# Pieces of eviction queued by step, an output product begun inside attention, and three buffers for the merge rows

## The chip, the cores and the metric

The kernel runs on one core of a Trainium2 chip. The core has five engines that work side by side and wait for each other by semaphores: TensorE (PE in the profile, its weight loads PEld), VectorE (DVE), ScalarE (ACT), GpSimd (POOL) and SyncE (SP), which here only issues DMAs, in order. The metric is device time of one execution in microseconds. Before the change the median of three runs is 2999.45 us (2996.9 to 3003.93).

## The reference

A trunk of two post-norm layers over a sequence of 1024 rows of width 1024, batch one, in float32. Each layer has a token mixer and then an MLP; each of these four sub-layers computes, for its input x,

```
h = x * (1 + scale) + shift          # shift, scale, gate from a conditioning vector c
x = LayerNorm(ALPHA * x + gate * f(h)) * ln_g + ln_b
```

The four functions f are, in order: a gated spatial mixer (`mixer_a`), an MLP `square(relu(h @ w_up)) @ w_down` with an inner width of 4096, attention (`mixer_b`), and a second MLP. Attention has 16 heads of 64 and three dilated patterns; each pattern gives an output and the logarithm of its softmax sum, and the three outputs of a head are added with the softmax of those logarithms as weights:

```
wts = softmax(stack(lses), axis=0)[..., None]
o = sum(wts * stack(outs), axis=0)
return o.reshape(B, S, H * E) @ w_out
```

## The kernel before

**Arithmetic.** Every float32 operand of a product is split into a rounded part and a rest (`split`, lines 102 and 103: a copy, mostly on ScalarE, then a subtraction, mostly on VectorE), and each product is three matmuls: hi·hi, hi·lo, lo·hi. A matmul has 128 rows of contraction, 128 columns of weights and up to 512 moving columns. A weight is loaded, multiplied by the gate row where it is an output weight (GpSimd, line 337), and split; that is a `unit`.

**Order of the work.** The program is written out in one order. The tile framework then orders the instructions of each engine by a simulated run with a cost for each, lowest position in the program first among those that are ready; an instruction can so be placed ahead of ones written before it, except those marked by `tc.keep_in_program_order`. Buffers come from pools: a tag has so many buffers, and a new tile waits until the old tile of its buffer has been released. SyncE's DMAs run in the order of its queue, and a DMA that waits for its source or its buffer holds those behind it.

**Output products** (`out_rows`, `rows_half`). The products of both mixers, `mixer_a` and attention, go through `out_rows`. The contraction of 1024 is cut in four chunks of two units, and the rows in two halves, which gives eight parts of 8 groups of 6 matmuls. The order of the parts (chunk, half) is (0,0), (0,1), (1,0), (1,1), (2,0), (3,0), (2,1), (3,1). A group of the first chunk is copied to the accumulator rows `acc` by ScalarE (line 367), a later one is added by VectorE (line 369). `add_x` adds the residual, `finish` does the LayerNorm of a row tile. The last part is interleaved with the building of the next sub-layer's input.

**MLP** (`mlp`). Both products use a scheme of seven half-size products in place of eight, numbered 1 to 7. The down products run in the order 2, 1, 5, 6, 3, 7, 4, each in eight steps of 24 matmuls. A step's operands are loaded (`load_step`, lines 861 and 872; one or two tiles of 512 KB from five buffers, two tagged `raw` and three tagged `res`) and split (`prepare`) into tiles from 13 buffers; the loads run two steps ahead and the splits one. Products 2, 5 and 3 accumulate in one set of four PSUM banks, 1, 6, 7 and 4 in another. After a product's last step its four banks are evicted at once (`evict`, lines 911 to 932): copies on ScalarE after 2, 5 and 6; on VectorE an addition (926), a multiplication by the gate (927) and an addition to the accumulator (930) after 1, 3 and 7; after 4 a multiplication (923) and an addition. After 3 and after 4 a row tile is complete and `finish` follows: statistics (240, 241), the reciprocal root (229 to 235), the normalization on ScalarE (245, 246), and for the MLPs the affine part with `ln_g` and `ln_b`: in the first MLP by GpSimd for six rows and VectorE for two (303, 304), in the second by GpSimd or VectorE (310 to 316), and a store (320). Product 4 ends row by row: its last two steps (four in the second MLP) are done for one bank after the other.

**Attention** (`attention`). `project` yields the projections q, k and v of 24 pairs (eight head pairs, three patterns) matmul group by matmul group; these are TensorE's filler. The attention itself stands in a table of 200 slots with three positions each, eight slots per head pair and pattern: scores, softmax, transposes and weighting. After each position two pieces of the projections follow. The projections end in slot 183; the last pattern occupies slots 184 to 191. `merge` combines the three patterns of a head pair: it reads the statistics back, computes the factors (1244 to 1256), writes them out, and reads them as rows broadcast over 64 partitions each (1272). The three rows of a merge share one buffer tagged `lng`, but in the last merge two have a tile of their own. Each is used to scale an output as soon as it is there (1273; on GpSimd for two of them, for one in the last merge), and two additions follow two slots later (1277, 1278). `attention_out` then opens its pools, loads the gate row (250), and calls `out_rows`; seven of the eight pairs' outputs come back from DRAM, the last is used where it is.

Of the kernel before, what the change touches and what calls it, by code (L numbers as in the profile page):

```python
# [10 lines left out]
F32 = mybir.dt.float32  # L11
F32R = mybir.dt.float32r
AF = mybir.ActivationFunctionType
ALU = mybir.AluOpType
# [22 lines left out]
def trunk(ctx: ExitStack, tc: tile.TileContext, x, c, ada_w, ada_b, ln_g, ln_b, a_w_in, a_b_in,  # L37
# [217 lines left out]
    class Residual:  # L255
# [3 lines left out]
        def __init__(self, j, stack):  # L259
            self.j = j  # L260
            halves = [pool(stack, f"acc{j}_{half}", 1, side="right") for half in (1, 0)][::-1]
            self.acc = [halves[i // 4].tile([P, D], F32, name=f"acc_{j}_{i}") for i in range(NT)]
            self.hT = []

# [22 lines left out]
        def finish(self, i):  # L287
# [7 lines left out]
            if j in (0, 2):  # L295
                nc.sync.dma_start(spill[j][i * P : (i + 1) * P, :], z)
            if j in (1, 3):
                if i == 0:
                    self.affine(j)
                xo = work.tile([P, D], F32, name=f"xo_{j}_{i}", tag="res", bufs=3)  # L300
                if j == 1:
                    e = G if i < 6 else V
                    e.tensor_tensor(xo[:], z, self.g[:], op=ALU.mult)
                    e.tensor_tensor(xo[:], xo[:], self.b[:], op=ALU.add)
                else:
                    cut = CUT[i]
                    w, v = slice(0, cut), slice(cut, D)
                    if cut < D:
                        normalize(z[:, v], mv[:, 0:1], mv[:, 2:3], mv[:, 3:4])
                        G.tensor_tensor(xo[:, v], z[:, v], self.g[:, v], op=ALU.mult)  # L310
                        G.tensor_tensor(xo[:, v], xo[:, v], self.b[:, v], op=ALU.add)
                    if cut:
                        V.scalar_tensor_tensor(xo[:, w], z[:, w], mv[:, 0:1], self.g[:, w], ALU.subtract, ALU.mult)  # L313
                    for w in [slice(0, HALF), slice(HALF, D)] if i == NT - 1 else [w]:
                        if cut:
                            V.scalar_tensor_tensor(xo[:, w], xo[:, w], mv[:, 2:3], self.b[:, w], ALU.mult, ALU.add)  # L316
                        if i == NT - 1:
                            nc.sync.dma_start(y_out[i * P : (i + 1) * P, w], xo[:, w])
                if j == 1 or i < NT - 1:
# [55 lines left out]
    def out_rows(stat, weight, gate, res, prepare, name):  # L375
# [15 lines left out]
        for i in (0, 1):  # L391
            res.add_x(i)
# [968 lines left out]
```

## Time and profile before

| | us |
|---|---|
| median of three runs | 2999.45 |
| the profiled execution | 3002.11 |
| its span, first to last instruction | 3000.4 |
| TensorE busy (matmuls) | 2795.7 |
| VectorE busy | 1968.7 |
| ScalarE busy | 1416.5 |
| GpSimd busy | 241.7 |
| mean granted TensorE clock | 0.969 |

The rows of a profile are read so. A timeline row has the start and the length in us, the engine and line, the operation, the written tile <- the read tiles, the shape, how many instructions were merged into the row, and in brackets how long the engine had been idle before it and who released it. A row of windows has the busy time of each engine with the number of its instructions, the granted clock of TensorE as a share of full speed, and the DMA's share and rate. SPq rows are DMA issues; their length includes the waiting of the queue. Names have no buffer numbers. The phases lie at: first mixer 0 to 365 us, first MLP up to 686 and down to 1039, attention 1039 to 2200, output product 2227 to 2327, second MLP to the end.

### The profile page before, as it was taken

The numbers are of one execution on the slowest core, as the hardware profiler recorded it, in microseconds if no ns is written. First come the engines' busy times: TensorE is split into PE (matmuls) and PEld (weight loads), VectorE is DVE, ScalarE is ACT, GpSimd is POOL, SyncE is SP. The second block draws the span as 40 slices with busy tenths as digits, with TensorE's granted clock in tenths as the row PEclk, the third lists the DMA queues.
The fourth block names the chain that finished last, engine by engine and source line by source line (L and its number), as shares of the span: only waits on it lengthen the run. The fifth ranks groups of instructions, "written<-read, shape, count | busy, mean of one in ns | idle before, by whom it ended". The sixth has DMA issues, their size and how long they took to land. (4 is left out here: it accounts for less than half of the span.)

```text
span 3000.4 us, 36904 instructions
## 1 busy us (share of the span) xinstructions
PE 2795.7 (93%) x13290; PEld 2296.6 (77%) x13290; DVE 1968.7 (66%) x3495; ACT 1416.5 (47%) x2617; POOL 241.7 (8%) x174
## 2 busy tenths in 40 slices
PE   6999999999997989999999999999859999999976
PEld 5777878887885768787878787878747788878865
DVE  6776897777847855555555555555458976577477
ACT  3234375554343345454545554545443755553432
POOL 1021000000002110101010101011011000000011
PEclk9999999999998999999999999999979999999988
DMA  7533356669624321212222222122143564495342
GB/s 246 162 99 114 118 179 212 219 217 335 231 94 139 126 72 30 65 37 65 36 58 37 65 37 58 41 56 48 29 117 128 172 209 148 147 320 197 94 156 96
DMA packets 322843, 375.77 MB, mean 125 GB/s; under 512 B 72236, under 2 KB 197588, under 8 KB 322660
## 3 DMA queue, kind: packets, MB, share of 16 engines
q1 hardware_dynamic: 322660, 373.41, 40.1%
q8 instruction: 104, 1.70, 0.3%
q14 instruction: 79, 0.65, 0.1%
HBM read 293.57 MB, written 79.77 MB: 124 GB/s over the span
## 5 line engine op out<-in xcount | busy, mean ns | idle before, releaser
L907 PE MATMUL psd<-rhi,lhi 128*128 128x512 f32 x896 | 355.9, 399 | 40.1 <-ACT rhi L102 37.9
L753 PE MATMUL psua<-right,left 128*128 128x512 f32 x1536 | 366.4, 392 | 0.0
L907 PE MATMUL psd<-rlo,lhi 128*128 128x512 f32 x896 | 356.8, 398 | 3.5 <-DVE rlo L103 3.3
L907 PE MATMUL psd<-rhi,llo 128*128 128x512 f32 x896 | 356.6, 398 | 0.0
L753 PEld LDWEIGHTS psua<-right,left 128*128 128x128 f32 x1536 | 287.6, 188 | 64.9 <-DVE right L103 0.9
L1057 PE MATMUL psv<-hT,wv_hi 128*128 128x512 f32 x768 | 258.2, 418 | 33.5 <-DVE k L103 21.2
L1135 ACT ACTIVATE p<-p,stat 128x128 f32<-128x128 f32 (+1 forms) x384 | 170.1, 444 | 217.9 <-DVE stat L1133 213.1
L1057 PE MATMUL psq<-hT,wq_hi 128*128 128x512 f32 x768 | 247.5, 403 | 0.0
L1057 PE MATMUL psk<-hT,wk_hi 128*128 128x512 f32 x768 | 246.9, 402 | 0.0
L907 PEld LDWEIGHTS psd<-rhi,lhi 128*128 128x128 f32 x896 | 169.6, 190 | 82.0 <-ACT rhi L102 39.0
L103 DVE TENSOR_TENSOR pTlo<-pT,pThi 128x512 fp32r<-128x512 f32 (+1 forms) x160 | 98.2, 621 | 187.4 <-ACT pThi L102 182.2
L103 DVE TENSOR_TENSOR llo<-lraw,lhi 128x1024 fp32r<-128x1024 f32 x112 | 139.0, 1241 | 115.1 <-PE psd L907 78.4
L907 PEld LDWEIGHTS psd<-rlo,lhi 128*128 128x128 f32 x896 | 170.0, 190 | 47.4 <-DVE rlo L103 7.3
L102 ACT CAST lhi<-lraw 128x1024 fp32r<-128x1024 f32 x112 | 117.6, 1050 | 180.4 <-PE psd L907 120.3
L907 PEld LDWEIGHTS psd<-rhi,llo 128*128 128x128 f32 x896 | 169.9, 190 | 39.6
L753 PE MATMUL psuc<-right,left 128*128 128x512 f32 x768 | 193.3, 397 | 1.1 <-ACT right L102 0.7
L1057 PEld LDWEIGHTS psv<-hT,wv_hi 128*128 128x128 f32 x768 | 139.6, 199 | 57.1 <-issue 36.8
L128 DVE SCALAR_TENSOR_TENSOR adaacc<-adaw,silu_c,adaacc 128x512 f32<-128x512 f32 x168 | 132.8, 800 | 62.4 <-DMA adaw<-in_ada_w_dram 61.4
L753 PEld LDWEIGHTS psuc<-right,left 128*128 128x128 f32 x768 | 143.4, 188 | 35.5 <-DVE right L103 1.2
L1199 DVE TENSOR_TENSOR oT<-oT,pv 64x512 f32<-64x512 f32 x96 | 89.5, 938 | 111.7 <-ACT oT L1198 111.1
L1057 PE MATMUL psv<-hT,wv_lo 128*128 128x512 f32 x384 | 156.9, 409 | 0.0
L1057 PE MATMUL psk<-hT,wk_lo 128*128 128x512 f32 x384 | 151.2, 394 | 2.3 <-DVE r L234 2.3
(255 smaller groups left out, 5937.8 us busy)
## 6 DMA issues: line engine op xcount, KB each, us to landing
lraw<-forms SPq DMA_DIRECT2D x112, 512.0 KB
adaw<-in_ada_w_dram SPq DMA_DIRECT2D x192, 256.0 KB
up<-in_mlp_w_up_dram SPq DMA_DIRECT2D x64, 512.0 KB
forms<-s SPq DMA_DIRECT2D x128, 256.0 KB
rraw<-in_mlp_w_down_dram SPq DMA_DIRECT2D x64, 512.0 KB
forms<-part SPq DMA_DIRECT2D x96, 256.0 KB
wq_raw<-in_b_w_qkv_dram SPq DMA_DIRECT2D x24, 512.0 KB
wk_raw<-in_b_w_qkv_dram SPq DMA_DIRECT2D x24, 512.0 KB
```

Of the source, the lines that this page charges most:

```text
L102: first = A.copy(hi, src) if hi_engine is A else hi_engine.tensor_copy(hi, src)
L103: return first, lo_engine.tensor_tensor(lo, src, hi, op=ALU.subtract)
L128: ins = V.scalar_tensor_tensor(acc[:], raw[:], silu_c[:, k : k + 1], acc[:], ALU.mult, ALU.add)
L753: T.matmul(acc, w[:, a, k, :], right[p][:, b, k, :], start=p in (1, 2, 5) and k + a + b == 0, stop=k == 3 and a == 1, skip_group_check=True)
L907: T.matmul(sums[kind, m][:], l[a][:, k, m * P : (m + 1) * P], r[b][:, k, :], start=p in (1, 2, 5) and kp + k + a + b == 0, stop=kp == KP - ...
L1057: T.matmul(p[:], wu[a][:, k * P : (k + 1) * P], hT[half][b][:, k, :], start=k + c_ == 0, stop=k == KD - 1 and c_ == 2)
L1135: A.activation(pr[:, 0:w], pr[:, 0:w], AF.Exp, bias=nm, scale=-1.0, accum_out=l)
L1199: V.tensor_tensor(dst, dst, sb, op=ALU.add)
```

## The change

- **Down products.** `evict` returns the part that follows the reading of PSUM as a function. After products 1 and 3 the four evictions, and after 3 also the four `finish` calls, go into a queue `due`, of which one piece is taken after each step; after 7 the four reads of PSUM are done at once and the rests are queued. A step's matmuls are written ahead of the loads and splits for later steps. Loads run three steps ahead, splits two. There are 14 split buffers for 13; the pool of half-row tiles is opened anew for the down part, with 14 for 16. The first MLP's product 4 leaves one step, not two, for the row by row end.
- **Affine part of the first MLP.** `finish` stores the normalized row only. In attention, in slots 2, 4, ... 16, `affine_row` reads a row tile back, multiplies and adds on GpSimd, and stores it.
- **Output product.** `out_rows` becomes the class `OutRows`. `begin` is the parts (0,0) and (1,0); `go_on` is (0,1), (1,1), (2,0), (3,0), (2,1). In attention, once the projections have ended, the last pattern's slots take pieces of `begin` in their place; the gate row is loaded at the start of attention; the first four accumulator rows lie in the buffers of q and k. `mixer_a` calls both in turn.
- **Merge.** The tag `lng` has three buffers. `spread` only issues the broadcasts; the scales and additions stand one per position in the following slots, one scale on GpSimd and two on VectorE.

```diff
-            last_kps = 4 if j == 3 else 2
+            last_kps = 4 if j == 3 else 1
-            LOADS, SPLITS = 2, 1
+            LOADS, SPLITS = 3, 2
+            due = deque()
...
+                    if p != 4 or kp < tail:
+                        matmuls(p, kp)
+                    if kp == KP - 1 and p != 4:
+                        if p in (1, 3):
+                            due.extend(lambda p=p, m=m: evict(p, m)() for m in range(4))
+                        else:
+                            rests = [evict(p, m) for m in range(4)]
+                            due.extend(rests if p == 7 else ())
+                        if p == 3:
+                            due.extend(lambda i=i: res.finish(i) for i in range(4))
                     if n + LOADS < len(steps):
                         load_step(*steps[n + LOADS])
                     if n + SPLITS < len(steps):
                         prepare(*steps[n + SPLITS])
-                    if p == 4 and kp >= tail:
-                        continue
-                    matmuls(p, kp)
                     if p in (2, 1) and kp % 2 and n < 2 * NT:
                         res.begin_x(n // 2)
-                    if kp == KP - 1:
-                        for m in range(4):
-                            evict(p, m)
-                    for _ in range(2):
-                        next(between, None)
+                    elif due:
+                        due.popleft()()
+                    if p == 4 and kp > 0:
+                        for _ in range(2):
+                            next(between, None)
...
+            def affine_row(i):
+                if i == 0:
+                    for n, src in (("g", ln_g), ("b", ln_b)):
+                        affine[n] = row_bc(f"aff_{n}")
+                        nc.sync.dma_start(affine[n][:], src[0, 1].partition_broadcast(P))
+                t = row_bc(f"aff_{i}")
+                rows = spill[1][i * P : (i + 1) * P, :]
+                nc.sync.dma_start(t[:], rows)
+                G.tensor_tensor(t[:], t[:], affine["g"][:], op=ALU.mult)
+                G.tensor_tensor(t[:], t[:], affine["b"][:], op=ALU.add)
+                nc.sync.dma_start(rows, t[:])
+
+            for i in range(NT):
+                at(2 + 2 * i, 1)(lambda i=i: affine_row(i))
...
+            def row_bc(name):
+                return vec.tile([P, S], F32, name=name, tag="lng", bufs=3)
...
                     for g in (1, 2, 0):
-                            bc = vec.tile([P, S], F32, name=f"bc_{hp}_{g}", tag="lng")
+                        bc = box[g] = row_bc(f"bc_{hp}_{g}")
                         for e in range(2):
                             nc.sync.dma_start(bc[64 * e : 64 * e + 64, :], w_dram[hp, g, e].partition_broadcast(64))
-                        (G if g == 1 or g and not at_end else V).tensor_tensor(oTs[g][:], oTs[g][:], bc[:], op=ALU.mult)
...
+                for n, f in enumerate((lambda: scale(1, G), lambda: scale(2, V), lambda: scale(0, V), lambda: add(1), lambda: add(2))):
+                    at(base + 2 + (n + 2) // 3, (n + 2) % 3)(f)
...
+            def output():
+                box["oT"] = [act_pair(f"oTs_{half}") for half in range(2)]
+                res = Residual(2)
+                for i in range(4):
+                    res.acc[i] = qk.tile([P, D], F32, name=f"acc_2_{i}", tag=("q0", "q1", "k0", "k1")[i])
+                out = box["out"] = OutRows(box["oT"], b_w_out[0], gate, res, prepare, "wo")
+                for ch in range(2):
+                    out.load(ch)
+                    prepare(ch)
+                box["begin"] = out.begin()
...
+                    for _ in range(2):
+                        if next(stream, True) and n >= last_group:
+                            if not box:
+                                output()
+                            fill = box["begin"]
+                            next(fill, None)
```

More of the change, by code (lines that the diff above doesn't have):

```diff
@@ L294, in finish @@
                 normalize(z, mv[:, 0:1], mv[:, 2:3], mv[:, 3:4])
-            if j in (0, 2):
+            if j < 3:
                 nc.sync.dma_start(spill[j][i * P : (i + 1) * P, :], z)
[L297 to L319, printed above, removed]
-                    nc.sync.dma_start((spill[1] if j == 1 else y_out)[i * P : (i + 1) * P, :], xo[:])
@@ L325, in build @@
                 self.hT.append(pair)
-                yield from build_hT(self.j + 1, half, [t[:] for t in self.acc[4 * half : 4 * half + 4]], pair, pinned=True)
+                yield from build_hT(self.j + 1, half, [t[:] for t in self.rows(half)], pair, pinned=True)
     def unit(src, name, gate=None, pinned=False, lo_engine=V, to=None):
@@ new lines, in trunk, with __init__, load, part @@
+    class OutRows:
+        def __init__(self, stat, weight, gate, res, prepare, name):
+            self.units = {}
+            def load(ch):
+                self.units[ch] = [unit(weight[k * P : (k + 1) * P, :], f"{name}_{k}", gate, ch > 1) for k in (2 * ch, 2 * ch + 1)]
+            def part(ch, half):
+                terms = [(stat[half], 2 * ch + n, self.units[ch][n]) for n in range(2)]
+                return rows_half(terms, res, ch == 0, ch == 3, half, f"{name}{ch}")
+            def last(between):
+                for _ in part(3, 1):
+                    next(between, None)
+                run(between)
+            self.load, self.part, self.prepare, self.res = load, part, prepare, res
+            res.last = last
+        def begin(self):
+            yield from self.part(0, 0)
+            yield from self.part(1, 0)
+        def go_on(self):
+            def part(*args):
+                run(self.part(*args))
+            def add(*rows):
+                for i in rows:
+                    self.res.add_x(i)
+            part(0, 1)
+            self.prepare(2)
+            self.load(2)
+            add(0, 1)
+            part(1, 1)
+            add(2, 3)
+            part(2, 0)
+            self.prepare(3)
+            self.load(3)
+            add(4, 5)
+            part(3, 0)
+            add(6, 7)
+            part(2, 1)
@@ L981, in attention @@
             vec = pool(ph, "vecB", 1)
+            gate = row_tile(gate_dram[2], "gate_2", "gate")
+            ql = pool(ph, "attn_qlo", 1)
             qk = pool(ph, "attn_qk", 2)
             qp = pool(ph, "attn", 2)
[L984 removed]
+            qlo = [[ql.tile([P, S], F32R, name=f"qlo{e}_{b}") for b in range(2)] for e in range(2)]
             for e in range(2):
```

171 lines of the change are left out of this document (84 added, 87 removed).

## The prediction

> **What bounds the kernel now.** I read the page first, then the windows (busy time of each engine in a stretch), the waits, and the timeline around the longest idle stretches of TensorE.
>
> ```profile
> PE 2795.7 (93%) x13290; PEld 2296.6 (77%) x13290; DVE 1968.7 (66%) x3495; ACT 1416.5 (47%) x2617; POOL 241.7 (8%) x174
> ```
>
> TensorE is busy for 2795.7 of 3000.4 us. So the time is TensorE's work plus its idle stretches, and, behind each, the time for which its granted clock is lower. The windows below hold every long idle stretch that the change touches, and two stretches for comparison. The columns are the width, then busy us and instructions of PE, PEld, DVE, ACT and POOL, the granted clock, the DMA share and GB/s.
>
> ```profile
> 930.00:960.00 30.00, 8.95 (x31) 6.42 (x30) 21.91 (x20) 7.32 (x9) 19.10 (x8) 0.66 0.49 175
> 1042.00:1072.00 30.00, 15.41 (x62) 12.06 (x61) 23.40 (x32) 9.26 (x12) 13.86 (x9) 0.77 0.37 122
> 1256.00:1276.00 20.00, 13.55 (x53) 10.22 (x52) 9.04 (x20) 6.41 (x18) 0.00 (x0) 0.74 0.30 80
> 1400.00:1416.00 16.00, 9.87 (x41) 7.40 (x40) 8.14 (x19) 5.95 (x17) 0.00 (x0) 0.89 0.31 90
> 1540.00:1556.00 16.00, 10.19 (x43) 7.67 (x42) 9.09 (x21) 5.84 (x16) 0.00 (x0) 0.89 0.35 98
> 1682.00:1696.00 14.00, 9.05 (x37) 6.64 (x36) 8.04 (x17) 5.08 (x14) 0.00 (x0) 0.88 0.24 77
> 1822.00:1840.00 18.00, 12.49 (x47) 9.38 (x47) 8.07 (x17) 6.08 (x17) 0.00 (x0) 0.72 0.26 71
> 1964.00:1982.00 18.00, 12.78 (x47) 9.45 (x46) 8.85 (x20) 6.21 (x17) 0.00 (x0) 0.72 0.32 86
> 2108.00:2126.00 18.00, 11.60 (x46) 8.88 (x46) 8.06 (x17) 5.08 (x14) 0.00 (x0) 0.81 0.27 87
> 2168.00:2236.00 68.00, 32.37 (x167) 25.98 (x166) 37.38 (x85) 29.14 (x74) 8.36 (x4) 0.72 0.42 87
> 2874.00:2902.00 28.00, 11.05 (x38) 8.10 (x37) 24.77 (x27) 7.25 (x9) 10.74 (x4) 0.70 0.53 187
> ...
> 1280.00:1400.00 120.00, 120.00 (x658) 102.21 (x657) 65.21 (x159) 63.80 (x155) 14.69 (x14) 1.00 0.21 47
> 2650.00:2700.00 50.00, 50.00 (x217) 40.44 (x216) 39.72 (x35) 23.33 (x25) 0.00 (x0) 1.00 0.94 321
> ```
>
> I price a window as its idle time plus its busy time times (1 - clock). That gives 24.1 us (21.05 + 8.95 x 0.34) at 930, where the first MLP's down products pass from product 3 to product 7; 18.1 at 1042, where that MLP passes to attention; 10.0, 7.2, 6.9, 6.0, 9.0, 8.8 and 8.6, together 56.5, at the seven merges; 44.7 (35.63 + 32.37 x 0.28) at 2168, from attention to the output product; and 20.3 at 2874, the second MLP's product 3 to 7. The sum is 163.7 us, the most that closing these gaps can give. Between merges TensorE shows no idle time at all, with VectorE at 65 and ScalarE at 64 of 120 us, so nothing else stands close behind it there.
>
> **Part A, the merge rows.** Three broadcast rows now share one buffer:
>
> ```profile
> 1240.21 1.16 SPq L1272 DMA_DIRECT2D bc<-w_dram  x2
> ...
> 1247.82 8.35 SPq L1272 DMA_DIRECT2D bc<-w_dram  x4
> ```
> ```profile
> 1252.51 2.39 POOL L1273 TENSOR_TENSOR oT<-oT,bc 128x1024 f32<-128x1024 f32 x1 [3.23 <-DMA bc<-w_dram]
> ```
> ```profile
> 1260.93 1.23 DVE L1273 TENSOR_TENSOR oT<-oT,bc 128x1024 f32<-128x1024 f32 x1 [3.91 <-DMA bc<-w_dram]
> 1262.19 0.69 DVE L103 TENSOR_TENSOR k<-psk,k 64x512 fp32r<-64x512 f32 x1
> ```
> ```profile
> 1263.03 0.70 PE L1057 MATMUL psv<-hT,wv_hi 128*128 128x512 f32 x2 [3.69 <-DVE k L103]
> ```
>
> The last row's broadcast goes out only after GpSimd has used the second; VectorE waits for it in order, the k eviction stands behind it, and TensorE waits for that. With three buffers all six half-row DMAs go out from 1240.2; at 0.6 us each they are issued by 1244. A landing takes 4.7 us (1247.82 to 1252.51), so the last lands near 1249, 12 us earlier. The scales and additions stand one position apart in later slots, and VectorE gets one scale of 1.23 us more per merge, GpSimd one less of 2.39; VectorE has 46% free there. I leave 1.2 us per merge, the added scale, for a landing that still comes late: 56.5 - 8.4 = **48 us gained**; bounds 28 (half of the stall stays) and 56.
>
> **Part B, the down products.** At 930 the chain is SyncE's queue:
>
> ```profile
> 935.25 9.76 SPq L320 DMA_DIRECT2D spill<-xo  x3
> 945.10 0.39 SPq L872 DMA_DIRECT2D rraw<-in_mlp_w_down_dram  x1
> ```
> ```profile
> 942.32 2.34 POOL L304 TENSOR_TENSOR xo<-xo,lnb 128x1024 f32<-128x1024 f32 x1
> 942.48 2.20 DVE L235 TENSOR_TENSOR mv<-r 128x1 f32<-128x1 f32 x1
> 944.71 0.16 DVE L245 SCALAR_TENSOR_TENSOR mv<-mv 128x1 f32<-128x1 f32 x1
> ...
> 953.26 1.22 PE L907 MATMUL psd<-rhi,lhi 128*128 128x512 f32 x2 [21.02 <-ACT rhi L102]
> ```
>
> Three stores of LayerNorm rows wait there for GpSimd's multiply and add, and the next weight load stands behind them for 9.8 us. Beside each GpSimd operation a VectorE operation of 0.15 us takes 2.2. In the first MLP the affine part leaves this place altogether, and the stores follow ScalarE's normalization. All evictions and finishes come one per step; a step is 24 matmuls of 50/217 = 0.230 us, 5.5 us, and the splits run two steps ahead where they ran one.
>
> ```profile
> 2869.45 0.64 DVE L926 TENSOR_TENSOR dpart<-psd,dpart 128x512 f32<-128x512 f32 x1
> ...
> 2870.86 0.69 DVE L930 TENSOR_TENSOR acc<-acc,dpart 128x512 f32<-128x512 f32 x1
> ...
> 2883.45 1.21 DVE L674 TENSOR_TENSOR rraw<-heldr,rraw 128x1024 f32<-128x1024 f32 x1
> 2884.97 1.28 DVE L313 SCALAR_TENSOR_TENSOR xo<-acc,mv,lng 128x1024 f32<-128x1024 f32 x1
> 2886.09 2.36 POOL L310 TENSOR_TENSOR xo<-acc,lng 128x1024 f32<-128x1024 f32 x1 [5.09 <-ACT acc L246]
> ```
>
> A step of product 7 costs VectorE a subtraction and two splits of about the same length, 3.6 us. An eviction adds three operations of these 512-wide forms, 0.64 + 0.64 + 0.69 = 2.0; a finish adds statistics, 2 x 0.69 estimated by the 512-wide row above, and some eight small operations at 0.15, 2.6 in all. First MLP: 8 x 3.6 + 4 x 2.0 + 4 x 2.6 = 47 us against 8 x 5.5 = 44; the excess of 3 lies under the two steps (11 us) of split reserve. I leave 4 us, so **20 gained**; bounds 12 and 24. Second MLP: two rows add 2 x 1.28 each on VectorE (5) and two rows add two GpSimd operations of 2.36 each (9.4 of possible blocking): up to 62 us against 44 + 11 of cover. I leave 6, so **14 gained**; bounds 6 and 20.
>
> **Part C, first MLP to attention.**
>
> ```profile
> 1056.69 2.75 DVE L304 TENSOR_TENSOR xo<-xo,lnb 128x1024 f32<-128x1024 f32 x2
> ...
> 1065.06 1.19 PE L1057 MATMUL psv<-hT,wv_hi 128*128 128x512 f32 x2 [12.29 <-DVE qlo L103]
> ```
>
> The evictions of q and k stand behind VectorE's affine rows (2.75 us for L304, about as much for L303) and small operations stretched by the four GpSimd operations of rows 4 and 5 (4 x 2.2 = 9 us by the row in Part B); both leave. Against that, the last product now keeps one step instead of two row by row, so the rows' LayerNorm starts about 4 us (half of a 24 x 0.230 step, plus the queue behind it) later. What is late next is the clearing of qlo behind the last row. 18.1 less 7: **11 gained**; bounds 3 and 17.
>
> **Part D, attention to output product.**
>
> ```profile
> 2211.08 0.58 SPq L250 DMA_DIRECT2D gate<-gate_dram  x1
> ```
> ```profile
> 2218.44 5.62 POOL L337 TENSOR_TENSOR wo_raw<-wo_raw,gate 128x1024 f32<-128x1024 f32 x2 [2.38 <-DMA gate<-gate_dram]
> ```
> ```profile
> 2227.31 1.22 PE L349 MATMUL psd_wo<-wo_hi,oTs 128*128 128x512 f32 x2 [26.72 <-ACT wo_hi L102]
> ```
>
> What ends the wait is the gate row: its DMA is issued behind the last merge's, and GpSimd's multiplication of the weights waits for it. The gate is now loaded at attention's start, and two of the eight parts (2 x 48 x 0.230 = 22 us) are offered to TensorE after the last projection. TensorE then holds this work while the last pattern and merge run. The first two chunks' preparation moves with them onto engines that the last pattern needs: 4 weight multiplications of 2.4 us on GpSimd; on VectorE 4 x 1.23 + 8 x 0.69 of splits and 8 x 0.69 of evictions, 16 us by the rows of these widths above, and about as much on ScalarE, where the 68 us of the window hold 37 of VectorE and 29 of ScalarE. The rest of the output product waits for its second half's accumulators, whose space the attention's small tiles leave only near the merge. Of 44.7 I take 28 (22 of filled work, and most of the clock's 9.1 less stalls): **28 gained**; bounds 10 and 42.
>
> **Part E, what is added.** Eight rows are read back, multiplied, added and stored during the first 18 of 200 slots: 16 GpSimd operations of 2.4 us, 38 us, where TensorE has no reserve but VectorE has. What they block:
>
> ```profile
> L103 DVE TENSOR_TENSOR k<-psk,k x96: 683/688/694, 1063.5 to 2158.9; 64x512 fp32r<-64x512 f32 x96
> ...
> L103 DVE TENSOR_TENSOR wv_lo<-wv_raw,wv_hi x24: 1210/1226/3226, 1047.5 to 2103.6; 128x1024 fp32r<-128x1024 f32 x24
> ```
>
> (min/median/max ns.) Evictions from PSUM never stretched, weight splits from SBUF did, and those run units ahead. Their 16 DMAs of 512 KB stand in SyncE's queue, each store behind GpSimd and each next weight load behind the store; 65 us of VectorE in 120 leave room. I take **3 lost**; bounds 12 lost and 0. The Trainium skill's page SBUF — State Buffer (section "SBUF: two separate sides") speaks against this move: a GpSimd operation and a VectorE one with two SBUF inputs exclude each other for a whole instruction. The rows above agree, for the splits alone. By the rule on every operation the term would be the fourth rival's.
>
> The first mixer's output product takes its parts in another order; its second pair of weights must be split one part (48 x 0.230 = 11 us) earlier:
>
> ```profile
> 278.08 1.22 DVE L103 TENSOR_TENSOR wout_lo<-wout_raw,wout_hi 128x1024 fp32r<-128x1024 f32 x1
> ```
> ```profile
> L349 PE MATMUL psd_wout<-wout_hi,uzT x256: 388/389/481, 274.7 to 364.7; 128*128 128x512 f32 x128
> ```
>
> The fourth weight is split at 279.3, and the first part, begun at 274.7, ends at 285.7: it costs nothing, and 11 us at most without that cover.
>
> **Sum.** 48 + 20 + 14 + 11 + 28 - 3 = 118 us. The profiled execution took 3002.1 us (span 3000.4), 2.7 above the median of the three runs shown; 3002.1 - 118 = 2884, and 2.7 less is 2881 for a median. I say **2882**.
>
> **Rivals.**
> 1. The last pattern slows as much as it is filled: VectorE, ScalarE and GpSimd serve both, and the chain of scores, exponent, transpose and weighting has no spare engine. For it: 37 + 16 + 10 us (GpSimd's four multiplications) of VectorE in 68; against it: the 27 us of wait inside those 68. Part D gives 10: 2900.
> 2. The merge's landing, not the buffer, decides: six DMAs together land later than two, and VectorE still waits in order. Against it stands the free DMA (0.30). Part A gives 24: 2906.
> 3. The planner already chose VectorE's order, so queuing one piece per step changes nothing but names, and product 7 is bound by VectorE (62 against 44 us). Part B gives 12 instead of 34: 2904.
> 4. GpSimd's 38 us of rows hit TensorE in full (against it: the k row): Part E loses 38: 2917.
> 5. Slower: raw tiles. There are five (two, and three shared with other rows), and products 2, 5, 7 and 4 take two per step, so three steps ahead ask for six. SyncE then waits in order for a free one. TensorE stalls once a tile's life from issue to split passes 2.5 steps, 13.8 us; at 18.7 us each of the 64 such steps loses (18.7 - 13.8)/2.5 = 2.0 us, 126 in all: 3010. From about 18.4 us the change loses. Against it: the second MLP's product 2 (2650 to 2700 above) is 50 of 50 busy today on the same five tiles.
>
> **How the numbers follow.** Forecast 0.52, rivals 0.18, 0.13, 0.09, 0.04 and 0.04. The range, 2848 to 2935, holds rivals 1 to 4 and, below, C and D at their best and A and B near it; all low bounds together would give 2955, all high ones 2840. Within 0.2% (6 us) is about what a measurement cannot tell from no change. Faster 0.94, same 0.02, slower 0.04.
>
> **What would show it.** A: no PE wait behind DVE k at the merges, clock 1.00 there, bc landings overlapping. B: no SP store wait of 9 us, PE idle under 6 us at products 3 to 7. C: psv's wait near 4 us. D: wo matmuls among the last pattern's, and none waiting 26 us. E: GpSimd rows of 2.4 us early in attention with TensorE at 9 tenths. Merge gaps of 5 us again, or idle time spread over the down products, would make the forecast wrong.

## The result, and the profile after

The changed kernel takes 2885.89 us, median of four runs (2883.73 to 2890.96), beside 2998.63 for the kernel before on the same chip: a ratio of 0.962, 95% interval 0.960 to 0.964, or about 113 us less. The profiled execution took 2883.92 us, its span 2881.8; against the profiled execution before (3002.11 us, 3.5 above its median) that is 118.6 us less of span. So the differences by stage below add up to some 6 us more than the medians do. Engines and their busy time, from the page of the changed kernel:

```profile
PE 2770.1 (96%) x13290; PEld 2280.9 (79%) x13290; DVE 1940.0 (67%) x3498; ACT 1415.6 (49%) x2617; POOL 235.6 (8%) x171
```

The matmuls are the same 13290. TensorE's span without matmuls fell from 3000.4 - 2795.7 = 204.7 us to 2881.8 - 2770.1 = 111.7, and 25.6 us of busy time went too, since less of it runs at a low clock (0.988 granted on average, 0.969 before).

To say where the time went I use the first or last matmul of each product as a mark. The rows are those of one tile in the kernel before, then in the changed one; the two times in each are the first and the last start.

```profile
L907 PE MATMUL psd<-rhi,lhi x896: 387/395/793, 690.8 to 2975.7; 128*128 128x512 f32 x180
...
L1057 PE MATMUL psq<-hT,wq_hi x768: 387/393/481, 1039.1 to 2141.9; 128*128 128x512 f32 x192
...
L1057 PE MATMUL psv<-hT,wv_lo x384: 387/393/632, 1066.0 to 2172.8; 128*128 128x512 f32 x192
...
L349 PE MATMUL psd_wo<-wo_hi,oTs x256: 387/389/794, 2227.3 to 2324.6; 128*128 128x512 f32 x128
```
```profile
L935 PE MATMUL psd<-rhi,lhi x896: 387/397/767, 685.6 to 2858.2; 128*128 128x512 f32 x180
...
L1101 PE MATMUL psq<-hT,wq_hi x768: 387/393/478, 1006.7 to 2044.1; 128*128 128x512 f32 x192
...
L1101 PE MATMUL psv<-hT,wv_lo x384: 388/393/628, 1020.8 to 2075.1; 128*128 128x512 f32 x192
...
L354 PE MATMUL psd_wo<-wo_hi,oTs x256: 387/389/792, 2077.8 to 2217.1; 128*128 128x512 f32 x128
```

| stage, from mark to mark | before | after | difference | forecast |
|---|---|---|---|---|
| start to the first psd (first mixer, up product) | 690.8 | 685.6 | -5.2 | 0 |
| to the first psq (down products, first MLP) | 348.3 | 321.1 | -27.2 | -20 (B) |
| to the last psv (attention) | 1133.7 | 1068.4 | -65.3 | -56 (A 48, C 11, E -3) |
| to the last psd_wo (end of attention, output product) | 151.8 | 142.0 | -9.8 | -28 (D) |
| to the last psd (second MLP) | 651.1 | 641.1 | -10.0 | -14 (B) |
| to the end | 24.7 | 23.6 | -1.1 | 0 |
| sum | 3000.4 | 2881.8 | -118.6 | -118 |

The total is as forecast; the parts are not. The mark at the first psq is a soft one. In the profiles of six runs below whose first MLP is the changed kernel's, that stage takes 322.1 to 326.4 us, and what it takes longer comes back in attention: in the four of them with the same attention up to its last pair, the two stages together take 1389.0 to 1390.9, as the changed kernel's 1389.5. So the split between these two rows is good to some 5 us.

The places of the long waits, in windows of the changed kernel (width, busy us of PE, PEld, DVE, ACT, POOL, granted clock, DMA share, GB/s):

```profile
900.00:960.00 60.00, 60.00 (x259) 48.43 (x259) 48.83 (x83) 26.84 (x30) 0.00 (x0) 1.00 0.66 219
1008.00:1028.00 20.00, 17.48 (x77) 13.99 (x76) 14.72 (x48) 10.01 (x16) 0.95 (x1) 0.91 0.71 238
1100.00:1170.00 70.00, 66.11 (x356) 54.94 (x355) 36.63 (x88) 37.51 (x90) 15.72 (x12) 1.00 0.50 62
1200.00:2060.00 860.00, 855.55 (x4647) 724.96 (x4646) 488.56 (x1180) 467.40 (x1117) 93.06 (x88) 1.00 0.24 54
2084.00:2112.00 28.00, 11.12 (x43) 8.85 (x44) 8.12 (x13) 10.06 (x19) 2.34 (x1) 0.70 0.56 72
2796.00:2822.00 26.00, 18.87 (x72) 14.84 (x71) 24.81 (x23) 8.48 (x9) 6.61 (x2) 0.87 0.71 225
```

The passage from product 3 to 7 of the first MLP is full (60 of 60, from 24.1 us lost). The seven merges together leave 4.45 us of idle time in 860, at full clock, from 56.5 lost. The entry of attention loses 4.1 (2.52 idle + 17.48 x 0.09), from 18.1. Two long waits are left: one of 16.9 us idle ahead of the output product, at a clock of 0.70, and one of 7.1 in the second MLP.

The first of them is where the forecast failed. Here are SyncE's waits, then ScalarE's, GpSimd's and TensorE's timeline rows around it (each a view of the changed kernel):

```profile
SPq L1283 <- DMA st_dram<-stat: 17.1, 1, 17.1
```
```profile
2077.69 0.34 SPq L337 DMA_DIRECT2D wo_raw<-in_b_w_out_dram  x1
2078.83 1.30 SPq L1267 DMA_DIRECT2D st_dram<-stat  x2
2080.23 0.87 SPq L337 DMA_DIRECT2D wo_raw<-in_b_w_out_dram  x1
2098.32 0.38 SPq L1283 DMA_DIRECT2D mst<-st_dram  x1
```
```profile
2100.86 2.34 POOL L342 TENSOR_TENSOR wo_raw<-wo_raw,gate 128x1024 f32<-128x1024 f32 x1 [17.24 <-issue]
```
```profile
2103.23 1.04 ACT L102 CAST wo_hi<-wo_raw 128x1024 fp32r<-128x1024 f32 x1 [16.34 <-POOL wo_raw L342]
2104.18 0.58 ACT L372 COPY acc<-psd_wo 128x512 f32<-128x512 f32 x1
```
```profile
2104.81 0.79 PE L354 MATMUL psd_wo<-wo_hi,oTs 128*128 128x512 f32 x1 [15.65 <-ACT acc L372]
```

TensorE waits for an accumulator copy; that copy stands in ScalarE's order behind the cast of a weight; the cast waits for GpSimd's multiplication; and the multiplication waits for a weight of 512 KB that was asked for at 2080.23, at once behind two stores of softmax statistics, and is used only at 2100.86. (The row of the multiplication names no releaser, only "issue"; that it waits for this load is read from the times.) Each of the two stores is 4 KB in 1,024 packets of 4 bytes, and SyncE waits 17.1 us for them to land. Meanwhile the DMA engines are busy and move little, and from 2089 on all other engines stand still:

```profile
DMA packets 2897, 1.19 MB, mean 52 GB/s; under 512 B 2612, under 2 KB 2612, under 8 KB 2897
```
```profile
2088.00:2092.00 4.00, 1.16 (x5) 0.59 (x4) 0.00 (x0) 0.00 (x0) 0.00 (x0) 1.00 0.81 26
2092.00:2096.00 4.00, 0.00 (x0) 0.00 (x0) 0.00 (x0) 0.00 (x0) 0.00 (x0) 0.64 0.80 31
```

(The first row is the DMA view from 2078 to 2101.) What fills the DMA engines there is not the stores. This is the DMA view from 2083 to 2098:

```profile
DMA packets 112, 0.43 MB, mean 29 GB/s; under 512 B 7, under 2 KB 7, under 8 KB 112
```

Nearly all of these are the weight's own packets of 4 KB. The load does not stand still behind the stores; it moves at 29 GB/s until they have landed. An earlier merge shows that the landing takes this long without any load behind the stores. They go out at 1273.77 and 1274.51; here are SyncE's wait for them and the DMA engines' busy share, in tenths, in 40 slices from 1273 to 1292:

```profile
SPq L1283 <- DMA st_dram<-stat: 16.6, 1, 16.6
DMA  0269999600000000000000000000000000000000
```

The DMA engines are idle from 1277 on, and the stores land some 15 us later. What they wait for in that time no run shows.

The kernel before issues the same stores, at 2176.51, with the next work of SyncE at 2195.57; there they lay under the wait for the gate row.

### The profile page after: what moved, and what is told of

It is laid out like the page before. It is cut to its first block, busy times and chain, and to the rows that moved or that the text cites. A ratio compares the mean times of both kernels' runs of the same rounds, so it can differ in the third digit from the quotient of the medians.

```text
span 2881.8 us, 36980 instructions
## 1 busy us (share of the span) xinstructions
PE 2770.1 (96%) x13290; PEld 2280.9 (79%) x13290; DVE 1940.0 (67%) x3498; ACT 1415.6 (49%) x2617; POOL 235.6 (8%) x171
## 4 chain that ended last, share of the span: by engine, by line
PE 77%; DVE 10%; DMA 6%; ACT 2%; issue 2%; POOL 2%; SPq 0%; another core or an unknown queue 0%; DVEq 0%; POOLq 0%; ACTq 0%
PE psd L935 20%; PE psua L780 11%; PE psq L1101 8%; PE psv L1101 8%; PE psk L1101 7%; PE psuc L780 6%; PE psd_wout L354 3%; PE psub L780 3%; PE pv L1228 2%; DMA adaw<-in_ada_w_dram 2%; PE sc L1175 1%; PE pT L1205 1%; PE sc L1174 1%; PE psu L354 1%; PE psd_wo L354 1%
## 5 line engine op out<-in xcount | busy, mean ns | idle before, releaser
L1101 PE MATMUL psv<-hT,wv_hi 128*128 128x512 f32 x768 | 246.8, 402 | 2.5 <-DVE qlo L103 2.5
L1101 PE MATMUL psq<-hT,wq_lo 128*128 128x512 f32 x384 | 151.8, 395 | 0.0
L1101 PEld LDWEIGHTS psv<-hT,wv_hi 128*128 128x128 f32 x768 | 133.5, 190 | 22.6 <-issue 3.1
L1101 PEld LDWEIGHTS psk<-hT,wk_hi 128*128 128x128 f32 x768 | 133.5, 189 | 19.9
```

What stands on the lines that cost most here:

```text
L1101: T.matmul(p[:], wu[a][:, k * P : (k + 1) * P], hT[half][b][:, k, :], start=k + c_ == 0, stop=k == KD - 1 and c_ == 2)
```

## The experiments

The theory at the start: the buffers carry A; the queue of one piece per step and the deeper reserve carry B; the move of the scale and offset carries C; and D is held up by the packets of the statistics. The rivals are those of the prediction. Where one run is given, it is one time, beside 2883.7 to 2891.0 for the changed kernel's four. The runs were made on several chips, on which the kernel before has medians of 2996.2 to 3000.2 us, so 4 us between the times of two runs say nothing.

### Part A alone, and the buffers alone

In the kernel before, the broadcast rows get three buffers; in the first run also the scales and additions stand one per position, as in the changed kernel; in the second nothing else is changed.

```diff
-bc = vec.tile([P, S], F32, name=f"bc_{hp}_{g}", tag="lng")
+bc = vec.tile([P, S], F32, name=f"bc_{hp}_{g}", tag="lng", bufs=3)
```

> The kernel before, with the change to the merge rows alone (three buffers, broadcasts issued together, scales and additions one per position). Theory: the seven merge stalls, priced at 56 us, go altogether: 2998.6 falls to 2943 (2938 to 2950), and no merge window has more than 1 us of idle TensorE. Rival (the landing decides, not the buffer): about 24 us, 2975.

> The kernel before, with three buffers for the merge rows and nothing else: each scale still stands right behind its broadcast, the two additions two slots later. Theory (the buffer held the broadcasts back): nearly the same gain as with the new positions, 45 to 56 us, 2943 to 2954. Rival (VectorE's scale stands too early in its queue and waits there for the landing): less than 25 us, above 2974.

Measured: 2937.55 and 2937.12 us, one run each, beside a median of 2996.27 before: 58.7 and 59.2 less, which is more than either theory gave. From the windows of the second:

```profile
1250.00:1276.00 26.00, 26.00 (x146) 22.26 (x145) 14.80 (x35) 15.30 (x35) 0.41 (x1) 1.00 0.21 63
...
1200.00:2090.00 890.00, 887.43 (x4834) 753.61 (x4833) 496.19 (x1228) 484.15 (x1159) 103.53 (x94) 1.00 0.23 53
```

The merges are full, with 2.6 us idle in 890. The buffers are the whole of A, and the new positions are worth nothing that one run each can tell. Six broadcasts issued together are no slower than needed, so the second rival falls.

### The statistics later, by their written place

```diff
-                @at(base + 8, 0)
+                @at(base + (12 if n == len(order) - 2 else 8), 0)
                 def statistics():
```

> The changed kernel, with one step moved: the statistics of the last head pair's second pattern are written to DRAM four slots later (slot 188 in place of 184). Theory (scattered packets): in the changed kernel the weight load issued at 2080.2 us lands only near 2100 because the statistics written beside it go out as some 2000 packets of 4 bytes; GpSimd, ScalarE and TensorE wait in a row. With the statistics later the idle stretch of 16.9 us at 2084 and about 2 us of lower clock go, and the time falls from 2886 to 2867 us (2862 to 2874). Rival (the engines of the last pattern are full): the stall only moves, and the time stays at 2880 or above.

Measured: 2883.35 us (2878.57 to 2884.61), ratio 0.961 (0.960 to 0.963), which overlaps the changed kernel's. The edit had no effect: the stores still went out at 2081 us, since the planner of the instruction order takes what is ready, and a written place is only a rank among ready things. So the run says nothing on the packets.

### The output product begun behind attention

```diff
                             fill = box["begin"]
-                            next(fill, None)
+                            if n >= len(slots):
+                                next(fill, None)
```

> The changed kernel, but the parts (0,0) and (1,0) of the output product are written behind the whole of attention, while weights and operands are still loaded and split in its last slots. Theory: the 22 us of filled matmuls lose their place beside the last pattern, but the 17 us stall of the weight load loses what it blocks (ScalarE's queue still waits for the weight): 2886 + 5 to 15 = 2891 to 2901. Rival (the fill is eaten up by the slower pattern): 2886 within 4 us.

Measured: 2880.61 us, one run: not 5 to 15 us above the changed kernel, as the theory had it, but 5 below, a little more than the rival allowed. The first psd_wo matmul still starts at 2080.7, as the planner puts it beside the last pattern wherever it is written. The written place of the fill gains nothing: from the last psv to the last psd_wo this run takes 136.0 us, the changed kernel 142.0. What part D gains comes from its other edits (the gate row, the weights and the accumulators early), which were not tried one by one.

### The stores pinned behind the loads, and the weights first

The four stores of the last pair but one are held in program order behind the loads; in the second run the first weights are also written ahead of the operands.

```diff
-                @at(base + 8, 0)
+                @at(base + (12 if n == len(order) - 2 else 8), 0)
...
-                                nc.sync.dma_start(d[s_, e]...
+                                ins = nc.sync.dma_start(d[s_, e]...
+                                if n == len(order) - 2:
+                                    tc.keep_in_program_order(ins)
```
```diff
-                for ch in range(2):
-                    out.load(ch)
-                    prepare(ch)
+                out.load(0)
+                out.load(1)
+                prepare(0)
+                prepare(1)
```

> The changed kernel, with the four scattered stores of the statistics of the last pair but one held in program order on the DMA queue, behind the loads of the first weights and operands of the output product (in the run with the later written place they had stayed ahead of them, at 2081 us). Theory: the 17 us in which TensorE waits for ScalarE's cast at 2084-2106 are the 2,096 packets of 4 bytes standing ahead of the 4 KB packets of the weights; with them behind, the weights land in about 2 us as everywhere else, the wait falls to under 4 us, the half clock that follows it (17 us, worth about 8) goes too, and the time is 2862-2872. Rival 1: the last pattern's engines are full, the weights are early but the casts of ScalarE still come behind the pattern's work: the wait stays over 12 us, time 2880-2888. Rival 2: the scatter now stands ahead of the next operands instead, and the wait only moves by some us to a later product: 2876-2884.

> The same as the run with the pinned stores, and the two first weight loads of the output product written ahead of the loads of its operands, whose two buffers held the weights back until 2077 us. Theory: the weights are cast some 20 us earlier, beside the last pattern, and nothing of the 17 us is left: 2858-2868, 2 to 6 us below the run with the pinned stores alone. Rival: the operands now come last, and TensorE waits for them as it had for the weights: within 2 us of the run with the pinned stores, or slower.

Measured: 2889.23 us (2883.12 to 2891.66) and 2882.93 (2878.99 to 2885.72); ratios 0.964 (0.962 to 0.966) and 0.962 (0.960 to 0.963). Neither differs measurably from the changed kernel, and neither theory came true. (The time of the first lies above the ranges of both its rivals, by 1 and by 5 us.) In the first, the weights are early and the wait at 2089 is gone, but a wait of the same length (16.5 us, from 2101.7) stands some 13 us later. ScalarE's longest wait in each (from 2085 to 2125):

```profile
ACT oTs L102 <- DMA oraw<-o_dram: 21.5, 3, 17.5
```
```profile
ACT oTs L102 <- DMA oraw<-o_dram: 18.6, 1, 18.6
```

Now the next operand stands behind the stores, and ScalarE, in order, waits for it. That is the second rival of the first run by its mechanism, though with its full price and not "some us". It speaks for the stores: whichever large transfer is behind them is waited for, for 17 to 19 us.

### The statistics in a quarter of the packets

The middle pattern's statistics are first brought by two VectorE copies into the order in which they lie in DRAM. Each of the four stores then has 256 packets of 16 bytes; no place on a queue is changed.

```diff
+sP = qp.tile([P, 4, 2, 4], F32, name=f"statP_{hp}", tag="statP", bufs=1)
+for i_ in range(2):
+    V.tensor_copy(sP[:, :, i_, :], stat[:].rearrange("p s e (r i) -> p (s e) r i", i=2)[:, :, :, i_])
 for s_ in range(2):
     for e in range(2):
-        nc.sync.dma_start(d[s_, e].rearrange("(i q r) -> q r i", r=4, q=P), stat[:, s_, e, :]...)
+        nc.sync.dma_start(d[s_, e].rearrange("(i q r) -> q i r", r=4, q=P), sP[:, 2 * s_ + e])
```

> The changed kernel, with the statistics of each middle pattern brought by two small VectorE copies into the order in which they lie in DRAM, so that each of the four stores has 256 packets of 16 bytes instead of 1,024 of 4; nothing is moved on the queue. Theory: the number of packets is what holds up the transfers behind them (2,096 packets, 17 us), whichever stand there, weights in the changed kernel, operands in the two runs with the stores pinned. A quarter of the packets takes about 4 us: the wait of 15.7 us at 2088-2112 falls to under 5, and with it the half clock behind it (8.5 us at half, worth up to 8 of busy time at half speed): 2862-2872. Rival: the transfers wait for something else in the queue (the bytes, the landing that a later read waits for): the wait stays over 12 us and the time is 2881-2888.

Measured: 2865.60 us (2862.12 to 2869.46), ratio 0.956 (0.954 to 0.958): 20 us under the changed kernel (19 by the ratios), and the intervals do not touch. In its profile all four stores go out at 2072.4, SyncE waits 3.5 us for them and no longer 17.1, and TensorE's longest wait falls to 2.3 us. Rows from its windows, its DMA issues (the last number is us from issue to landing) and TensorE's waits from 2070 to 2125:

```profile
2084.00:2112.00 28.00, 24.58 (x130) 19.70 (x131) 21.42 (x54) 17.63 (x46) 4.97 (x2) 1.00 0.29 95
```
```profile
wo_raw<-in_b_w_out_dram SPq DMA_DIRECT2D x1, 512.0 KB, 5.8
```
```profile
SPq L1287 <- DMA st_dram<-statP: 3.5, 1, 3.5
```
```profile
PE psd_wo L354 <- ACT acc L372: 3.7, 2, 2.3
```

SyncE's waits for these stores over the whole run (the number of waits stands between the total and the longest) show the same at every merge, first in the changed kernel, then here, where a middle pattern's tile is called statP:

```profile
SPq L1283 <- DMA st_dram<-stat: 139.8, 17, 18.3
```
```profile
SPq L1287 <- DMA st_dram<-statP: 24.7, 11, 3.7
SPq L1287 <- DMA st_dram<-stat: 15.0, 8, 3.0
```

So the form of the stores, 4-byte packets in this number, is the cause of the wait. The bytes are the same, and four stores, not two, now stand right ahead of the weight. Whether it is the number or the smallness of the packets was not tried. By the marks, 14.9 of the 20 us come from the last psv to the last psd_wo (127.1 us) and 5.1 from the first MLP and attention together (1384.4).

### Without the scale and offset rows in attention

```diff
-                at(2 + 2 * i, 1)(lambda i=i: affine_row(i))
+                pass
```

> The changed kernel without the eight rows of scale and offset on GpSimd early in the attention (the scale and offset of the first MLP's LayerNorm are left out of the computation). Theory: the rows run beside TensorE and cost the few idle stretches that the profile shows between 1018 and 1168 us, 5.5 us together and no lower clock: 2878-2884. Rival: GpSimd's 38 us of rows stop VectorE's work of two operands and so TensorE in full: 2845-2855.

Measured: 2878.74 us, one run, 7.1 under the changed kernel's median. From 1100 to 1170 us, where the changed kernel's row above has 66.11 busy of 70, this one has

```profile
1100.00:1170.00 70.00, 70.00 (x386) 59.68 (x385) 40.29 (x94) 39.34 (x93) 6.26 (x7) 1.00 0.23 39
```

(The kernel leaves the scale and offset out of the computation.) On this run's chip the kernel before is 2.4 us faster too, so the rows cost some 4 us of idle time and at most 7, not 38: the fourth rival falls.

### The scale and offset back in the down product

```diff
+            if j == 1:
+                if i == 0:
+                    self.affine(j)
+                xo = work.tile([P, D], F32, name=f"xo_{j}_{i}", tag="res", bufs=3)
+                e = G if i < 6 else V
+                e.tensor_tensor(xo[:], z, self.g[:], op=ALU.mult)
+                e.tensor_tensor(xo[:], xo[:], self.b[:], op=ALU.add)
+                z = xo[:]
...
-                at(2 + 2 * i, 1)(lambda i=i: affine_row(i))
+                pass
```

> The changed kernel with the scale and offset of the first MLP's LayerNorm back in the rows of the down product (six on GpSimd, two on VectorE), and no rows of them in the attention. Theory: the queue of one piece per step gave the first MLP its 20-27 us, and the move of the scale and offset only the wait ahead of the attention, of which I gave 11 of 18 us: 2889-2902, with the product 3 to 7 of the first MLP as in the changed kernel within 5 us, and a TensorE gap of 6-16 us at 1000-1020 us. Rival 1: the move is most of what the first MLP gained: product 3 to 7 is 15 us or more longer than in the changed kernel, 2905-2915. Rival 2: it is worth nothing in either place: 2882-2887.

Measured: 2911.15 us, one run, 25 above the changed kernel. Two waits are back, TensorE's only long ones from 955 to 1062, one in the passage to product 7 and one at the entry of attention; then the windows around them:

```profile
PE psv L1109 <- DVE qlo L103: 17.2, 1, 17.2
PE psd L943 <- DVE dpart L963: 11.8, 1, 11.8
```
```profile
958.00:982.00 24.00, 12.15 (x39) 8.95 (x38) 22.81 (x19) 5.97 (x6) 9.28 (x4) 0.72 0.63 214
1034.00:1062.00 28.00, 10.78 (x43) 8.54 (x42) 18.16 (x24) 7.66 (x11) 10.25 (x8) 0.63 0.26 95
```

They cost 15.3 us (11.85 + 12.15 x 0.28) and 21.2 (17.22 + 10.78 x 0.37). So the first rival of this run holds. With the queue and the deeper reserve in place, 15 of the first MLP's 24 us stay lost as long as the affine operations stand there. From 955 to 972 four of VectorE's splits and sums, 1.22 us each elsewhere, take 3.36 to 3.45 beside GpSimd's, and VectorE is busy for 22.81 of 24 us.

### The two halves of the edit of the down products

```diff
-            LOADS, SPLITS = 3, 2
+            LOADS, SPLITS = 2, 1
```

> The changed kernel with the loads of the down products two steps ahead and the splits one, as they were, and the queue of one piece per step kept. Theory: the queue and the move of the scale and offset free the first MLP, and a step ahead less costs only where VectorE is full, at the passage from product 3 to 7 of the two MLPs: 2 to 6 us in each, 2888-2896. Rival 1: the depth carries part B: both gaps come back, 15 to 25 us in all: 2899-2910. Rival 2: three steps ahead are short of raw tiles and the shallower order frees them: 2876-2883.

and, in another kernel,

```diff
                     elif due:
                         due.popleft()()
+                    while due:
+                        due.popleft()()
```

> The changed kernel with the pieces (evictions, finishes) written at once at the end of each product and not one per step; depths and the place of the scale and offset as in the changed kernel. Theory: a bunch of eight evictions and finishes stands ahead of the next splits on VectorE, at the two passages from product 3 to 7 and at the entries of products 2 and 5: 8 to 15 us back, 2892-2902. Rival 1: the planner of the order spreads them by itself, since only the data bind it, and the queue is worth nothing: 2882-2888. Rival 2: without the queue both gaps are as before, 24 and 20 us: 2920-2930.

Measured: 2880.86 us with the shallower order, one run, below the changed kernel; and 2901.20 with all pieces written at once, one run, 15 above it. TensorE's longest wait in the second MLP, with the pieces at once and its two windows, then the same passage with the shallower order:

```profile
PE psd L935 <- ACT rhi L102: 18.3, 1, 18.3
```
```profile
706.00:724.00 18.00, 13.50 (x45) 10.73 (x44) 13.61 (x15) 9.86 (x10) 0.00 (x0) 0.72 0.90 318
...
2774.00:2802.00 28.00, 9.75 (x33) 7.31 (x33) 23.04 (x39) 7.12 (x10) 10.35 (x4) 0.63 0.47 170
```
```profile
2796.00:2820.00 24.00, 19.85 (x74) 14.44 (x73) 22.60 (x23) 8.46 (x9) 1.68 (x1) 0.93 0.70 241
```

Without the queue the second MLP has its old wait again (18.25 idle of 28; 16.95 before); the first MLP loses 4.5 us idle near 710, at a clock of 0.72 (3.2 idle of 20 in the changed kernel, at full clock), and nothing in its passage to product 7, which is full (60 of 60 from 900 to 960). So the queue is what the second MLP gains, and the deeper reserve adds nothing: that passage of the first MLP is full with the shallower order too.

The shallower order's time lies not in the theory's range but in the second rival's (2876 to 2883), and the deeper reserve does cost a little. The second MLP takes 639.0 us by the marks with the shallower order, and 638.3 in the next run, which has it too; in the eight profiles with the deeper order and the queue it takes 640.4 to 641.7. The fifth rival's 126 us do not show. SyncE does wait for raw tiles (line 889, 103.7 us in 27 waits in the second MLP), but with the shallower order it waits as long (101.5 in 26), and TensorE's one long wait there is the one of 7.1 us above.

### Packed statistics and the shallower order together

The edits of the packed statistics and of the shallower order, both.

> The changed kernel with the packed statistics and the shallower order of the down products together: loads two steps ahead, splits one. Theory: the two act in different places (the wait ahead of the output product, and the passage from product 3 to 7 of the second MLP, whose gap was 3.9 us with the shallower order alone where the changed kernel has 7.1) and add: 2865.6 less 3 to 6 us, 2858-2863. Rival: the 5 us of the shallower order were the scatter of a single run: 2863-2868.

Measured: 2863.61 us (2858.66 to 2864.21, five runs), ratio 0.954 (0.953 to 0.955). Beside the packed statistics alone, 0.956 (0.954 to 0.958), the intervals overlap; the time lies in the rival's range, 0.6 us above the theory's. The depth of the reserve makes no difference that the times of these runs can tell; by the marks it is the 2 us in the second MLP. Both kernels beat the changed one by some 20 us.

## Why the prediction was right or wrong

The predicted 2882 us and the direction are right: 2885.89 was measured, 113 us less by the medians and 118.6 by the profiles, where 118 was forecast. That the sum fits so well is luck, since two errors cancel. By the table, part D brought 18 us less than forecast and B's second MLP 4 less; the first MLP, attention and the stages that were put at nothing brought 23 more.

**A, right, its size too small.** The cause (one buffer, so the last broadcast waits for GpSimd) is shown by the run of the buffers alone. The term that was mis-sized is the 1.2 us that I left at each merge for a late landing, 8.4 in all: 4.45 us of idle time remain in all of 860, and 2.6 in 890 with the buffers alone. Alone the buffers gain 59 us, above my upper bound of 56, with one run each. In the changed kernel the attention stage gives 65.3 less C's 14.0 (18.1 - 4.1) plus E's 3.9, 55 us, good to the 5 us of its mark.

**B, first MLP, right in its sum and in one of its three causes.** The stage gained 27 (22 to 27 by the other profiles) and I had 20. I put the gain down to the stores that no longer wait for the affine part, to the queue and to the reserve together. The runs separate them in the passage to product 7. With the affine part moved away, leaving out the queue or the deeper reserve costs nothing there (they were not left out together). With it in its old place, both together save 9 of the 24 us, and 15 stay lost. So the move carries it. The 4 us that I left for VectorE's 47 against 44 were not paid.

**B, second MLP, right, a little too large.** It gained 10 against 14, and the queue is shown as the cause. I had left 6 us; the window at 2796 still loses 9.6 (7.13 + 18.87 x 0.13). The cause is the one that I named, GpSimd's two operations for each of two rows. These rows of VectorE and GpSimd in the changed kernel show it:

```profile
2797.19 3.44 DVE L103 TENSOR_TENSOR llo<-lraw,lhi 128x1024 fp32r<-128x1024 f32 x1
2800.55 3.44 DVE L701 TENSOR_TENSOR rraw<-rraw,heldt 128x1024 f32<-128x1024 f32 x1
...
2810.98 2.47 DVE L955 TENSOR_TENSOR dpart<-psd,dpart 128x512 f32<-128x512 f32 x4
```
```profile
2796.22 3.32 POOL L315 TENSOR_TENSOR xo<-acc,lng 128x1024 f32<-128x1024 f32 x1 [5.96 <-DVE rlo L103]
2799.62 3.29 POOL L316 TENSOR_TENSOR xo<-xo,lnb 128x1024 f32<-128x1024 f32 x1
```

A split and an operand's sum, 1.22 us each elsewhere, take 3.44 each beside them, 4.4 us more in all (2 x 2.22). The reads of PSUM, for which TensorE waits, stand behind them in VectorE's order.

**C, right.** 14.0 gained against 11; the run with the scale and offset back shows the cause, and its wait for qlo is the one that I had named as late next, at full price.

**D, the step that failed.** I gave 28: 22 of filled work, and most of the clock's loss. The step reads "TensorE then holds this work while the last pattern and merge run". It holds the work, but only until its fourth weight: the load of that one stands behind the stores of the statistics on the queue, at 2080, and the weight is now wanted at once. The step counts the work that moves onto GpSimd, VectorE and ScalarE, and puts the loads that this work waits for at nothing, whatever stands ahead of them. In the kernel before, the wait for the gate row had hidden those stores. TensorE waited 15.65 us for that weight, and the stage gained 9.8. That is the size of the first rival, but not its mechanism: it had the engines of the last pattern full, and the windows at 2088 to 2096 show VectorE, ScalarE and GpSimd at 0.00 us. With the packets cut to a quarter, most of the missing part comes back: the stage takes 127.1 us, which makes D 24.7 (151.8 - 127.1).

**E, right.** 3 forecast; 3.9 us idle in the profile, 7 in one run without the rows, of which the chips may make 2. The page SBUF — State Buffer of the Trainium skill, section "SBUF: two separate sides", has a GpSimd operation and a VectorE one with two SBUF inputs shut each other out. The rows of the second MLP above agree with it, and so does the move of the rows to attention: the eviction of k, which reads PSUM, keeps its 694 ns at most (min/median/max) there:

```profile
L103 DVE TENSOR_TENSOR k<-psk,k x96: 683/688/694, 1018.5 to 2061.1; 64x512 fp32r<-64x512 f32 x96
```

**Not in the sum.** The first mixer and the up product are 5.2 us shorter and the end 1.1. No run separates these. The fifth rival's 126 us on top of 2882 make 3008 and not 3010; nothing hangs on it.

## What to carry to other kernels

A transfer that is hidden today has a price that shows when the work beside it moves: before moving loads to an earlier place, read what is ahead of them on the DMA queue, in packets and in the time to landing, not in bytes. Where the planner takes what is ready first, a written place is no more than a wish; a buffer, a pinned order or less work changes something. A wait that moves with every edit of the order, and keeps its length, points at what it waits for and not at the order.

## What the hardware showed that was not expected

Two stores of 4 KB each, in 2,048 packets of 4 bytes, took 17.1 us to land. Their packets take little of the DMA engines: in an earlier merge the engines are idle for some 15 us before such stores have landed. But while they land, the weight load behind them moves slowly, at 26 to 37 GB/s and a share of 0.8, where the same engines move 347 GB/s at a share of 0.97 in the first MLP:

```profile
690.00:720.00 30.00, 26.82 (x119) 21.54 (x119) 23.02 (x25) 13.15 (x13) 0.00 (x0) 1.00 0.97 347
...
2084.00:2088.00 4.00, 2.77 (x16) 2.41 (x17) 2.33 (x2) 2.84 (x4) 0.00 (x0) 1.00 0.81 37
```

By the landing, that is 0.13 us for one packet of 4 bytes on its engine (17.1 x 16 / 2,048), an estimate that takes the packets as evenly spread over 16 engines. A 512 KB load issued behind them was usable 20.6 us after its issue (2080.23 to 2100.86), where 5.8 were enough behind the packed ones. The Trainium skill's page DMA: Bandwidth & Descriptors, section "Queues, rings and completion order", says that SyncE's DMAs share one ring on each DMA engine, which reads it in order. The trace agrees as far as the order goes: weights in the changed kernel and operands in the two runs with the stores pinned, whatever came next on SyncE's queue, was late. That the load's packets, once begun, are slow until the stores have landed is more than an order, and its cause stays open.
